# A two-block transformer layer on one core: the last product's second half of tokens delayed by two weight chunks, the norm's weights multiplied in during the product, two queues for the output, and the last expert and the gating unit written in another order

## The chip, the cores and the metric

One core of a Trainium2 chip runs the whole program in one launch. The metric is device time in microseconds (us), as the median of the runs shown. The engines are called PE (matmuls), DVE (vector), ACT (scalar, with function tables), POOL and SP; SP, ACT and POOL issue transfers (DMAs), each on a queue of its own.

## What is computed

Two transformer blocks in a row, on 256 tokens of width 2048, all in float32. The first block has four attention mixers and a mixture of 16 experts; the second a long convolution (hyena), a gating unit and a feed-forward part. The pieces that the change touches:

```python
# first block, experts: 4 groups of 4, each token in one group
y = (silu(h @ w_gate[e]) * (h @ w_up[e]) * weight[e]) @ w_down[e]      # D=2048, D_EXPERT=512

# second block, gating unit (D_SGU=1024, 8 heads, chunks of 128 tokens)
u, v = jnp.split(gelu(p), 2, axis=-1)
v = layernorm(v, ln_g, ln_b)
s = jnp.einsum('hpq,bnqhc->bnphc', w_s, v) + b_s
y_sgu = u * s

# the end
x = x + (silu(gate) * up) @ w_ffn_out       # D_FF=5632
return rmsnorm(x) * norm_final_g            # over the 2048 columns of a token
```

## The kernel before

Every large product is made of three matmuls in a 32-bit format with fewer mantissa bits (`mm3`, L160 to L162): a weight chunk of 128 x 1024 numbers is loaded on SP's queue (`rload`, L193, 512 KB), ACT makes its high part `whi` (L148), DVE the low part `wlo` (L151), and PE multiplies high by high, high by low and low by high. Loads go into a ring of five buffers (`wraw`), the parts into rings of three each (`nsplit`). Products of form "C" have the weights stationary and give columns by tokens; those of form "T" have the tokens stationary and give 128 tokens by 512 columns.

The text of the kernel is not the order of execution: a planner goes through the instructions by priority (their place in the text) and by when it expects their inputs, and writes one list for each engine. It takes a later instruction first where an earlier one isn't ready by its reckoning. On the chip each engine then follows its list strictly.

**Experts** (`experts`, L1149 on). For each of 16 experts: the gate product (8 chunks, `widen(wg)`), Silu, then the down product of the expert before (`down()`, 8 chunks, two halves of 1024 columns), then the up product (8 chunks), gate times up times weight (L1179), four transposes (L1182) and the split of the result. After the last expert its own `down()` follows at once.

**Gating unit** (`sgu`, L1575 on). ACT's queue loads the norm's weights `lg`, `lb`, the bias `bs` (each broadcast to 128 partitions, 512 KB) and `ws`. Two T products give v, with Gelu (L1590) and statistics (L1591). In the text there follow the eight transposes of `ws` (L1596), the root and the norm of v in passes over 1024 columns (L1605 to L1607), then two C products for u, and for each head the small products with `v` (L1616).

**The end** (`block2`, L1377, from L1454). `xt` holds the residual with tokens on partitions, `gb` the broadcast weights of the last norm. The product with `w_ffn_out` runs in four quarters of 512 columns; in a quarter each of its 22 chunks (two row blocks of weights) is multiplied for both halves of 128 tokens at once. After a quarter DVE adds (L1469) and ACT squares with a sum (L1471). After the fourth the root is taken (L1476), DVE multiplies by root and weights in eight passes of 512 columns (L1481), and SP stores each (L1482, 256 KB).

Of the kernel before, what the change touches and what calls it, by code (L numbers as in the profile page):

```python
# [9 lines left out]
F32 = mybir.dt.float32  # L10
F32R = mybir.dt.float32r
I32 = mybir.dt.int32
AF = mybir.ActivationFunctionType
# [5 lines left out]
P = 128  # L19
S = 256  # L20
D = 2048
KD = D // P
# [119 lines left out]
class Body:  # L142
# [53 lines left out]
    def wload(self, src, kt, width, perm=False):  # L196
# [9 lines left out]
        h = self.wp.tile([P, 1024], F32R, name="whi", tag="whi", bufs=self.nsplit)  # L206
        l = self.wp.tile([P, 1024], F32R, name="wlo", tag="wlo", bufs=self.nsplit)
# [137 lines left out]
    def run(self):  # L345
        ctx, tc, nc, i = self.ctx, self.tc, self.nc, self.i
        self.nraw, self.nsplit = 5, 3
        self.ahead, self.turn, self.more, self.nada, self.alias, self.taken, self.first = {}, None, None, 0, {}, 0, True
        self.const = ctx.enter_context(tc.tile_pool(name="const", bufs=1, reuse_waits="tile"))
# [799 lines left out]
    def experts(self, groups, weights, step, finish, between=None):  # L1149
# [7 lines left out]
        for n in range(4 * len(groups)):  # L1157
# [18 lines left out]
            if down:  # L1176
                down()
            u = widen(wu, "u")
            nc.vector.scalar_tensor_tensor(he, sg, cs[:, e:e + 1], u, OP.mult, OP.mult)  # L1179
            pt = self.bank("b").rearrange("p (k s) -> p k s", k=4)  # L1180
            for k in range(4):
                nc.tensor.transpose(pt[:, k], he[:, k * P:(k + 1) * P], self.ident)  # L1182
            hh, hl = (midr[:, j].rearrange("p (k s) -> p k s", k=4) for j in range(2))
            self.split(hh, hl, pt)
# [3 lines left out]
            def down(e=e, hh=hh, hl=hl, wd=wd, y=y, take=take):  # L1188
# [4 lines left out]
                for half in range(2):  # L1193
                    for k in range(4):
                        wt = self.wload(src[4 * half + k], 1, 1024)
                        for q in range(2):
                            self.mm3(y[half * 2 + q], (hh[:, k], hl[:, k]), [t[:, 0, q * 512:(q + 1) * 512] for t in wt],
                                     e == 0 and k == 0, e == 3 and k == 3)
                        step()
# [177 lines left out]
    def block2(self):  # L1377
# [59 lines left out]
        with ExitStack() as cf:  # L1437
# [26 lines left out]
            ss = fp.tile([P, 2, 8], F32, name="fss")  # L1464
            T2 = [("T", 0, 512, 0), ("T", 0, 512, 1)]
            for q in range(4):
                cs = slice(q * 512, (q + 1) * 512)
                for a, p in enumerate(self.gemm(i["w_ffn_out_2"][0], KF, q * 512, 512, lambda k: (ah[:, k], al[:, k]), T2)):
                    nc.vector.tensor_tensor(xt[:, a, cs], xt[:, a, cs], p, OP.add)  # L1469
                    sq = fp.tile([P, 512], F32, name="fsq", tag="fsig", bufs=1)  # L1470
                    nc.scalar.activation(sq, xt[:, a, cs], AF.Square, accum_out=ss[:, a, q:q + 1])  # L1471
            for a in range(2):
# [6 lines left out]
                for q in range(4):  # L1479
                    cs = slice(q * 512, (q + 1) * 512)  # L1480
                    nc.vector.scalar_tensor_tensor(xt[:, a, cs], xt[:, a, cs], r[:, 6:7], gb[:, cs], OP.mult, OP.mult)  # L1481
                    nc.sync.dma_start(self.out[0, a * P:(a + 1) * P, cs], xt[:, a, cs])  # L1482
# [92 lines left out]
    def sgu(self, w, xs, C4):  # L1575
# [3 lines left out]
        nc.scalar.dma_start(lg, bc("sgu_ln_g_2", DH))  # L1579
        nc.scalar.dma_start(lb, bc("sgu_ln_b_2", DH))  # L1580
        nc.scalar.dma_start(bs, bc("sgu_b_s_2", DH))
# [11 lines left out]
        for h0 in (0, 4):  # L1593
            ps = self.bank("b").rearrange("p (h q) -> p h q", h=4)
            for h in range(4):
                nc.tensor.transpose(ps[:, h], ws[:, h0 + h], self.ident)  # L1596
            nc.vector.tensor_copy(wst[:, h0:h0 + 4], ps)
        for a in range(2):
            r = sp.tile([P, 8], F32, name="sr", tag="sr", bufs=2)
            nc.vector.bn_aggr(r[:, :2], st[:, a].rearrange("p h s -> p (h s)"))  # L1600
            nc.vector.tensor_scalar(r[:, 2:3], r[:, 1:2], EPS, None, OP.add)
            nc.scalar.activation(r[:, 3:4], r[:, 2:3], AF.Sqrt)
# [45 lines left out]
```

## Time and profile before

| | us |
|---|---|
| median of three runs (lowest, highest) | 2630.53 (2626.57, 2633.94) |
| the profiled execution | 2630.51 |
| its span, first to last instruction | 2628.4 |
| PE busy in the span | 2551.8 (97%) |
| DVE busy | 1788.6 (68%) |
| ACT busy | 1333.8 (51%) |

All times in the rows are microseconds from the span's start unless marked ns. A timeline row gives start, duration, engine, line, operation and tiles; a number in brackets is the engine's idle time before it and what ended that. Matmuls overlap in the pipeline, so the distance of two starts says more than a duration.

### The profile page before, as it was taken

How to read it: one execution, taken by the hardware profiler on the slowest of the kernel's cores; microseconds unless marked ns; L12 is line 12 of the kernel's file. 1: busy time of each engine (PE TensorE's matmuls, PEld its weight loads, DVE VectorE, ACT ScalarE, POOL GpSimd, SP SyncE). 2: the span in 40 equal slices, each digit the busy share in tenths (PEclk: the TensorE clock that was granted, in tenths of full speed). 3: DMA queues.
4: the chain of work that ended last, by engine and by line, in shares of the span. 5: the costliest groups of instructions: out<-in, count | busy, mean ns of one | idle time of the engine just before them, and what ended most of it. 6: DMA issues, size and time to landing. Idle time of an engine off the chain costs nothing.

```text
span 2628.4 us, 43630 instructions
## 1 busy us (share of the span) xinstructions
PE 2551.8 (97%) x17355; PEld 2246.0 (85%) x17355; DVE 1788.6 (68%) x2513; ACT 1333.8 (51%) x1774; POOL 7.3 (0%) x21
## 2 busy tenths in 40 slices
PE   6998999998999999999999999999999999999997
PEld 2476878897888878787997899999999999998886
DVE  5647768777999899997787655556655555555444
ACT  2333444545777777776444444445544444443443
POOL 0000000000000000000000000000000000000000
PEclk8998999998999999999999999999999999999999
DMA  9998889883899999996554555555565555555554
GB/s 362 335 300 289 283 308 328 307 312 114 314 340 322 341 341 375 342 374 248 190 167 129 169 185 185 190 187 184 187 192 189 188 188 189 188 190 196 195 193 137
DMA packets 320394, 640.81 MB, mean 244 GB/s; under 512 B 21748, under 2 KB 36116, under 8 KB 319416
## 3 DMA queue, kind: packets, MB, share of 16 engines
q1 hardware_dynamic: 310768, 618.83, 69.2%
q10 hardware_dynamic: 8392, 13.89, 1.6%
q0 software_dynamic: 1024, 5.25, 0.6%
q8 instruction: 137, 2.24, 0.3%
q14 instruction: 73, 0.60, 0.1%
HBM read 631.02 MB, written 6.35 MB: 242 GB/s over the span
## 4 chain that ended last, share of the span: by engine, by line
PE 72%; DVE 2%; ACT 1%; issue 1%; DMA 0%; ACTq 0%; DVEq 0%
PE ps_y L160 19%; PE ps_y L161 19%; PE ps_y L162 19%; PE ps_u L161 2%; PE ps_g L161 2%; PE ps_g L160 2%; PE ps_u L162 2%; PE ps_u L160 2%; PE ps_g L162 2%; DVE wlo L151 1%; PE ps_b L160 0%; PE ps_b L161 0%; PE ps_b L162 0%; DMA ws<-in_sgu_w_s_dram 0%; ACT whi L148 0%
## 5 line engine op out<-in xcount | busy, mean ns | idle before, releaser
L151 DVE TENSOR_TENSOR wlo<-wraw,whi 128x1024 fp32r<-128x1024 f32 (+1 forms) x972 | 1163.8, 1205 | 642.7 <-ACT whi L148 614.5
L148 ACT ACTIVATE whi<-wraw 128x1024 fp32r<-128x1024 f32 (+1 forms) x972 | 1011.2, 1045 | 923.6 <-PE ps_y L161 453.3
L160 PE MATMUL ps_y<-hH,whi 128*128 128x256 f32 x2432 | 684.2, 281 | 0.0
L162 PE MATMUL ps_y<-hH,wlo 128*128 128x256 f32 x2432 | 680.0, 280 | 0.0
L161 PE MATMUL ps_y<-hL,whi 128*128 128x256 f32 x2432 | 679.2, 279 | 0.0
L160 PEld LDWEIGHTS ps_y<-hH,whi 128*128 128x128 f32 x2432 | 457.8, 188 | 1.9 <-issue 1.7
L161 PEld LDWEIGHTS ps_y<-hL,whi 128*128 128x128 f32 x2432 | 457.8, 188 | 1.9 <-issue 1.7
L162 PEld LDWEIGHTS ps_y<-hH,wlo 128*128 128x128 f32 x2432 | 457.8, 188 | 1.5 <-issue 1.3
L160 PE MATMUL ps_mm<-hH,whi 128*128 128x256 f32 (+1 forms) x784 | 226.4, 289 | 4.7 <-ACT whi L148 4.7
L162 PE MATMUL ps_mm<-hH,wlo 128*128 128x256 f32 (+1 forms) x784 | 222.6, 286 | 2.2 <-DVE wlo L151 2.1
L161 PE MATMUL ps_mm<-hL,whi 128*128 128x256 f32 (+1 forms) x784 | 221.6, 283 | 0.0
L160 PEld LDWEIGHTS ps_mm<-hH,whi 128*128 128x128 f32 (+1 forms) x784 | 147.1, 188 | 24.8 <-issue 11.6
L162 PEld LDWEIGHTS ps_mm<-hH,wlo 128*128 128x128 f32 (+1 forms) x784 | 146.6, 188 | 10.3 <-DVE wlo L151 5.6
L161 PEld LDWEIGHTS ps_mm<-hL,whi 128*128 128x128 f32 (+1 forms) x784 | 147.2, 188 | 1.1 <-issue 0.6
L161 PE MATMUL ps_y<-wlo,actH 128*128 128x512 f32 x352 | 137.5, 390 | 0.0
L162 PE MATMUL ps_y<-whi,actL 128*128 128x512 f32 x352 | 137.3, 390 | 0.0
L160 PE MATMUL ps_y<-whi,actH 128*128 128x512 f32 x352 | 137.2, 390 | 0.0
L161 PE MATMUL ps_y<-wlo,piece 128*128 128x512 f32 x256 | 101.8, 398 | 0.3 <-DVE wlo L151 0.2
L162 PE MATMUL ps_y<-whi,piece 128*128 128x512 f32 x256 | 100.1, 392 | 0.3 <-DVE piece L151 0.3
L480 PE MATMUL ps_ada<-piece,cact 128*32 128x512 f32 x488 | 88.6, 641 | 5.1 <-DMA piece<-in_ada_w_dram 4.2
L160 PE MATMUL ps_y<-whi,piece 128*128 128x512 f32 x256 | 91.4, 392 | 0.7 <-ACT piece L148 0.7
L484 DVE SCALAR_TENSOR_TENSOR arow<-piece,cs,arow 128x512 f32<-128x512 f32 x120 | 89.5, 746 | 1.8 <-DMA piece<-in_ada_w_dram 0.8
(521 smaller groups left out, 3885.9 us busy)
## 6 DMA issues: line engine op xcount, KB each, us to landing
wraw<-in_w_in_dram SPq DMA_DIRECT2D x224, 512.0 KB, 4.2
piece<-in_ada_w_dram SPq DMA_DIRECT2D x186, 512.0 KB, 7.0
wraw<-in_w_ffn_in_dram SPq DMA_DIRECT2D x176, 512.0 KB, 4.5
wraw<-in_exp_w_down_dram SPq DMA_DIRECT2D x125, 512.0 KB, 5.6
wraw<-in_exp_w_up_dram SPq DMA_DIRECT2D x124, 512.0 KB, 5.5
wraw<-in_exp_w_gate_dram SPq DMA_DIRECT2D x122, 512.0 KB, 5.4
wraw<-in_w_ffn_out_dram SPq DMA_DIRECT2D x88, 512.0 KB, 4.2
wraw<-in_w_out_dram SPq DMA_DIRECT2D x64, 512.0 KB, 4.8
```

Of the source, the lines that this page charges most:

```text
L148: self.nc.scalar.activation(dst, src, AF.Copy)
L151: self.nc.vector.tensor_tensor(dst, src, h.bitcast(F32), OP.subtract)
L160: mm(ps, a[0], b[0], start=start, stop=False)
L161: mm(ps, a[0], b[1], start=False, stop=False)
L162: mm(ps, a[1], b[0], start=False, stop=stop)
L480: nc.tensor.matmul(ps[m:m + 32], self.cact[:, k], r, start=q == 0, stop=q == 3)
L484: nc.vector.scalar_tensor_tensor(sb, r, self.cs[:, k:k + 1], sb, OP.mult, OP.add)
```

## The change

It has four parts. In the gating unit the three broadcast loads move to POOL's queue, and root, norm of v and transposes of ws become a generator, one step of which is written behind each chunk of the first u product. For the last expert, the down product of the one before is written behind its up product, and the transposes and the split of the last expert's result behind two of that product's chunks. In the last quarter of the final product the second 128 tokens follow the first by two chunks, with two more buffers for each split part (`split_more`, taken for two chunks in five); the first 128 tokens are closed when their sum is complete. The weights of the last norm are multiplied in after each quarter, into `xg`, which lies where `xT` was; the close is one pass of 1024 columns on DVE and one on ACT, each stored from its own queue (SP, ACT). A root of no use is written ahead of the product.

```diff
@@ -203,8 +203,15 @@
         else:
             raw = self.ahead.pop(self.turn) if self.turn in self.ahead else self.rload(src, kt, n)
             self.turn += 1
-        h = self.wp.tile([P, 1024], F32R, name="whi", tag="whi", bufs=self.nsplit)
-        l = self.wp.tile([P, 1024], F32R, name="wlo", tag="wlo", bufs=self.nsplit)
+        pool, tag, bufs = self.wp, "", self.nsplit
+        if self.split_more:
+
+            here, at = self.split_more
+            self.split_more = here, (at + 1) % (bufs + 2)
+            if at < 2:
+                pool, tag, bufs = here, "2", 2
+        h = pool.tile([P, 1024], F32R, name="whi", tag="whi" + tag, bufs=bufs)
+        l = pool.tile([P, 1024], F32R, name="wlo", tag="wlo" + tag, bufs=bufs)
         if perm:
             for a in range(2):
                 g = lambda t, pat, **kw: t[:, :n].rearrange(pat, k=kt, a=2, i=4)
@@ -346,6 +353,7 @@
         ctx, tc, nc, i = self.ctx, self.tc, self.nc, self.i
         self.nraw, self.nsplit = 5, 3
         self.ahead, self.turn, self.more, self.nada, self.alias, self.taken, self.first = {}, None, None, 0, {}, 0, True
+        self.split_more = None
         self.const = ctx.enter_context(tc.tile_pool(name="const", bufs=1, reuse_waits="tile"))
         self.res = ctx.enter_context(tc.tile_pool(name="res", bufs=1, reuse_waits="tile"))
         self.wp = ctx.enter_context(tc.tile_pool(name="wts", bufs=1, reuse_waits="tile"))
@@ -1173,19 +1181,28 @@
                 mid, midr = (t.rearrange("p (a n) -> p a n", a=2) for t in between)
             sg, he = mid[:, 0], mid[:, 1]
             nc.scalar.activation(sg, g, AF.Silu)
-            if down:
+            hh, hl = (midr[:, j].rearrange("p (k s) -> p k s", k=4) for j in range(2))
+
+            def turned():
+                pt = self.bank("b").rearrange("p (k s) -> p k s", k=4)
+                for k in range(4):
+                    nc.tensor.transpose(pt[:, k], he[:, k * P:(k + 1) * P], self.ident)
+                self.split(hh, hl, pt)
+
+
+            ends = n == 4 * len(groups) - 1 and not between
+            if down and not ends:
                 down()
             u = widen(wu, "u")
             nc.vector.scalar_tensor_tensor(he, sg, cs[:, e:e + 1], u, OP.mult, OP.mult)
-            pt = self.bank("b").rearrange("p (k s) -> p k s", k=4)
-            for k in range(4):
-                nc.tensor.transpose(pt[:, k], he[:, k * P:(k + 1) * P], self.ident)
-            hh, hl = (midr[:, j].rearrange("p (k s) -> p k s", k=4) for j in range(2))
-            self.split(hh, hl, pt)
+            if ends:
+                down(midst=turned)
+            else:
+                turned()
             if e == 0:
                 y = []
 
-            def down(e=e, hh=hh, hl=hl, wd=wd, y=y, take=take):
+            def down(e=e, hh=hh, hl=hl, wd=wd, y=y, take=take, midst=None):
                 if e == 0:
                     finish()
                     y += [self.bank("y") for _ in range(4)]
@@ -1196,6 +1213,8 @@
                         for q in range(2):
                             self.mm3(y[half * 2 + q], (hh[:, k], hl[:, k]), [t[:, 0, q * 512:(q + 1) * 512] for t in wt],
                                      e == 0 and k == 0, e == 3 and k == 3)
+                        if midst and half == 0 and k == 1:
+                            midst()
                         step()
                     if e == 3:
                         take(half, y[2 * half:2 * half + 2])
@@ -1462,24 +1481,58 @@
                         nc.tensor.transpose(ps[:, kk * P:(kk + 1) * P], self.xT[:, q * 4 + kk, a * P:(a + 1) * P], self.ident)
                     nc.vector.tensor_copy(xt[:, a, q * 512:(q + 1) * 512], ps)
             ss = fp.tile([P, 2, 8], F32, name="fss")
+
+            nc.scalar.activation(ss[:, 0, 7:8], rB[:, 0:1], AF.Sqrt)
             T2 = [("T", 0, 512, 0), ("T", 0, 512, 1)]
-            for q in range(4):
-                cs = slice(q * 512, (q + 1) * 512)
-                for a, p in enumerate(self.gemm(i["w_ffn_out_2"][0], KF, q * 512, 512, lambda k: (ah[:, k], al[:, k]), T2)):
-                    nc.vector.tensor_tensor(xt[:, a, cs], xt[:, a, cs], p, OP.add)
-                    sq = fp.tile([P, 512], F32, name="fsq", tag="fsig", bufs=1)
-                    nc.scalar.activation(sq, xt[:, a, cs], AF.Square, accum_out=ss[:, a, q:q + 1])
-            for a in range(2):
+            wo, ks = i["w_ffn_out_2"][0], lambda k: (ah[:, k], al[:, k])
+
+            def add(q, a, p):
+
+                t = xt[:, a, q * 512:(q + 1) * 512]
+                nc.vector.tensor_tensor(t, t, p, OP.add)
+                sq = fp.tile([P, 512], F32, name="fsq", tag="fsig", bufs=1)
+                nc.scalar.activation(sq, t, AF.Square, accum_out=ss[:, a, q:q + 1])
+                nc.vector.tensor_tensor(xg[:, a, q * 512:(q + 1) * 512], t, gb[:, q * 512:(q + 1) * 512], OP.mult)
+
+            def close(a):
+
                 r = ss[:, a]
                 nc.vector.tensor_reduce(r[:, 4:5], r[:, :4], AX.X, OP.add)
                 nc.vector.tensor_scalar(r[:, 4:5], r[:, 4:5], 1.0 / D, EPS, OP.mult, OP.add)
                 nc.scalar.activation(r[:, 5:6], r[:, 4:5], AF.Sqrt)
                 nc.vector.reciprocal(r[:, 6:7], r[:, 5:6])
                 self.newton(r[:, 6:7], r[:, 4:5], r[:, 7:8])
-                for q in range(4):
-                    cs = slice(q * 512, (q + 1) * 512)
-                    nc.vector.scalar_tensor_tensor(xt[:, a, cs], xt[:, a, cs], r[:, 6:7], gb[:, cs], OP.mult, OP.mult)
-                    nc.sync.dma_start(self.out[0, a * P:(a + 1) * P, cs], xt[:, a, cs])
+                rows, cs = slice(a * P, (a + 1) * P), [slice(h * 1024, (h + 1) * 1024) for h in range(2)]
+                nc.vector.tensor_scalar(xg[:, a, cs[0]], xg[:, a, cs[0]], r[:, 6:7], None, OP.mult)
+                nc.sync.dma_start(self.out[0, rows, cs[0]], xg[:, a, cs[0]])
+                nc.scalar.activation(xg[:, a, cs[1]], xg[:, a, cs[1]], AF.Copy, scale=r[:, 6:7])
+                nc.scalar.dma_start(self.out[0, rows, cs[1]], xg[:, a, cs[1]])
+
+
+            xg = self.xT.rearrange("p k s -> p (k s)").rearrange("p (a d) -> p a d", a=2)
+            for q in range(3):
+                for a, p in enumerate(self.gemm(wo, KF, q * 512, 512, ks, T2)):
+                    add(q, a, p)
+
+            self.split_more = fp, 0
+            ps = self.accumulators(T2)
+            held = {}
+            for c in range(KF // 2 + 2):
+                if c < KF // 2:
+                    k0 = 2 * c
+                    held[c] = self.wload(wo[k0 * P:(k0 + 2) * P, 1536:].rearrange("(k p) n -> p k n", p=P), 2, 512)
+                for a, n in ((0, c), (1, c - 2)):
+                    if not 0 <= n < KF // 2:
+                        continue
+                    for kk in range(2):
+                        k = 2 * n + kk
+                        x = [t[:, a * P:(a + 1) * P] for t in ks(k)]
+                        self.mm3(ps[a], x, [t[:, kk] for t in held[n]], k == 0, k == KF - 1)
+                if c == KF // 2 - 1:
+                    add(3, 0, ps[0])
+                    close(0)
+            add(3, 1, ps[1])
+            close(1)
 
 
     def hyena(self, w, xs, C4):
@@ -1576,9 +1629,9 @@
         nc, sp, i = self.nc, self.sp, self.i
         bc = lambda nm, n: bass.AP(tensor=i[nm].tensor, offset=i[nm].offset, ap=[[0, P], [1, n]])
         lg, lb, bs = (sp.tile([P, DH], F32, name=n) for n in ("lng", "lnb", "sbs"))
-        nc.scalar.dma_start(lg, bc("sgu_ln_g_2", DH))
-        nc.scalar.dma_start(lb, bc("sgu_ln_b_2", DH))
-        nc.scalar.dma_start(bs, bc("sgu_b_s_2", DH))
+        nc.gpsimd.dma_start(lg, bc("sgu_ln_g_2", DH))
+        nc.gpsimd.dma_start(lb, bc("sgu_ln_b_2", DH))
+        nc.gpsimd.dma_start(bs, bc("sgu_b_s_2", DH))
         ws = sp.tile([P, 8, P], F32, name="ws")
         nc.scalar.dma_start(ws, i["sgu_w_s_2"][0].rearrange("h p q -> p h q"))
         v = sp.tile([P, 2, DH], F32, name="sv")
@@ -1590,23 +1643,36 @@
                 nc.scalar.activation(v[:, a, cs], p, AF.Gelu, scale=self.tr12[:, a:a + 1])
                 nc.vector.bn_stats(st[:, a, hf], v[:, a, cs])
         wst = sp.tile([P, 8, P], F32, name="wst")
-        for h0 in (0, 4):
-            ps = self.bank("b").rearrange("p (h q) -> p h q", h=4)
-            for h in range(4):
-                nc.tensor.transpose(ps[:, h], ws[:, h0 + h], self.ident)
-            nc.vector.tensor_copy(wst[:, h0:h0 + 4], ps)
-        for a in range(2):
-            r = sp.tile([P, 8], F32, name="sr", tag="sr", bufs=2)
-            nc.vector.bn_aggr(r[:, :2], st[:, a].rearrange("p h s -> p (h s)"))
-            nc.vector.tensor_scalar(r[:, 2:3], r[:, 1:2], EPS, None, OP.add)
-            nc.scalar.activation(r[:, 3:4], r[:, 2:3], AF.Sqrt)
-            nc.vector.reciprocal(r[:, 4:5], r[:, 3:4])
-            self.newton(r[:, 4:5], r[:, 2:3], r[:, 5:6])
-            nc.vector.tensor_scalar(v[:, a], v[:, a], r[:, 0:1], r[:, 4:5], OP.subtract, OP.mult)
-            nc.vector.tensor_tensor(v[:, a], v[:, a], lg, OP.mult)
-            nc.vector.tensor_tensor(v[:, a], v[:, a], lb, OP.add)
+
+        def chores():
+
+            rs = []
+            for a in range(2):
+                r = sp.tile([P, 8], F32, name="sr", tag="sr", bufs=2)
+                nc.vector.bn_aggr(r[:, :2], st[:, a].rearrange("p h s -> p (h s)"))
+                nc.vector.tensor_scalar(r[:, 2:3], r[:, 1:2], EPS, None, OP.add)
+                nc.scalar.activation(r[:, 3:4], r[:, 2:3], AF.Sqrt)
+                nc.vector.reciprocal(r[:, 4:5], r[:, 3:4])
+                self.newton(r[:, 4:5], r[:, 2:3], r[:, 5:6])
+                rs.append(r)
+            yield
+            for a in range(2):
+                nc.vector.tensor_scalar(v[:, a], v[:, a], rs[a][:, 0:1], rs[a][:, 4:5], OP.subtract, OP.mult)
+                nc.vector.tensor_tensor(v[:, a], v[:, a], lg, OP.mult)
+                yield
+                nc.vector.tensor_tensor(v[:, a], v[:, a], lb, OP.add)
+                yield
+            for h0 in (0, 4):
+                ps = self.bank("b").rearrange("p (h q) -> p h q", h=4)
+                for h in range(4):
+                    nc.tensor.transpose(ps[:, h], ws[:, h0 + h], self.ident)
+                nc.vector.tensor_copy(wst[:, h0:h0 + 4], ps)
+            yield
+        bg = chores()
         for hf in range(2):
-            for m, p in enumerate(self.gemm(w, KD, 3072 + hf * 512, 512, xs, C4)):
+            for m, p in enumerate(self.gemm(w, KD, 3072 + hf * 512, 512, xs, C4, lambda _: next(bg, None))):
+                if m == 0:
+                    self.drain(bg)
                 h = hf * 4 + m
                 u = sp.tile([P, S], F32, name="su", tag="su", bufs=2)
                 nc.vector.tensor_tensor(u, p, self.rB, OP.mult)
```

## Rows read from the trace of the kernel before

**Rows 1.** The page's first part: busy time, share of the span, instructions.

```profile
PE 2551.8 (97%) x17355; PEld 2246.0 (85%) x17355; DVE 1788.6 (68%) x2513; ACT 1333.8 (51%) x1774; POOL 7.3 (0%) x21
```

**Rows 2.** Waits of PE, whole span: waited for, us in total, times, longest.

```profile
PE ps_g L1596 <- DMA ws<-in_sgu_w_s_dram: 4.6, 1, 4.6
...
PE ps_g L1616 <- DVE sv L1607: 2.3, 1, 2.3
```

**Rows 3.** Timeline around the transposes of ws: start, duration, what, idle before.

```profile
1433.44 0.35 ACTq L1579 DMA_DIRECT2D lng<-in_sgu_ln_g_dram  x1
...
1434.79 0.57 ACTq L1583 DMA_DIRECT2D ws<-in_sgu_w_s_dram  x1
...
1445.46 1.12 PE L1596 MATMUL ps_g<-vec,ws 128*128 128x128 f32 x4 [4.58 <-DMA ws<-in_sgu_w_s_dram]
...
1446.62 0.69 DVE L1597 COPY wst<-ps_g 128x512 f32<-128x512 f32 x1 [7.69 <-PE ps_g L1596]
...
1451.31 0.39 PE L160 MATMUL ps_y<-whi,hH 128*128 128x512 f32 x1
```

**Rows 4.** DMA issues: count, KB each, median us from issue to landing.

```profile
wraw<-in_w_in_dram SPq DMA_DIRECT2D x224, 512.0 KB, 4.2
...
lng<-in_sgu_ln_g_dram ACTq DMA_DIRECT2D x1, 512.0 KB, 6.5
...
sbs<-in_sgu_b_s_dram ACTq DMA_DIRECT2D x1, 512.0 KB, 8.8
```

**Rows 5.** Window behind that wait: length, busy by engine, granted clock, DMA share, GB/s.

```profile
1445.00:1447.00 2.00, 1.53 (x7) 1.54 (x8) 0.38 (x1) 0.00 (x0) 0.00 (x0) 0.50 0.00 0
```

**Rows 6.** Timeline around the norm of v, and the later small products.

```profile
1469.32 1.54 DVE L1605 TENSOR_SCALAR sv<-sv,sr 128x1024 f32<-128x1024 f32 x2
...
1474.41 0.46 PE L1616 MATMUL ps_g<-wst,sv 128*128 128x128 f32 x2 [2.35 <-DVE sv L1607]
...
1478.23 0.28 PE L162 MATMUL ps_y<-hH,wlo 128*128 128x256 f32 x1
...
1516.63 0.61 PE L1616 MATMUL ps_u<-wst,sv 128*128 128x128 f32 x4
...
1518.33 0.36 PE L160 MATMUL ps_y<-hH,whi 128*128 128x256 f32 x1
```

**Rows 7.** Timeline of PE behind the last expert's up product.

```profile
1196.32 0.39 PE L162 MATMUL ps_u<-whi,piece 128*128 128x512 f32 x1
...
1197.55 0.66 PE L1182 MATMUL ps_b<-vec,piece 128*128 128x128 f32 x4 [0.84 <-DVE piece L1179]
...
1200.99 0.39 PE L160 MATMUL ps_y<-whi,piece 128*128 128x512 f32 x1
```

**Rows 8.** Timeline from the last matmul on.

```profile
2614.04 0.39 PE L162 MATMUL ps_y<-whi,actL 128*128 128x512 f32 x1
...
2615.98 1.28 ACT L1476 ACT_TABLE_LOAD   x1
...
2616.19 0.15 DVE L1475 TENSOR_SCALAR fss<-fss 128x1 f32<-128x1 f32 x1
2617.28 0.30 ACT L1476 ACTIVATE fss<-fss 128x1 f32<-128x1 f32 x2
...
2618.48 5.39 DVE L1481 SCALAR_TENSOR_TENSOR hH<-hH,fss,hL 128x512 f32<-128x512 f32 x8
```

**Rows 9.** Windows over the stores, columns as in rows 5.

```profile
2619.00:2620.00 1.00, 0.00 (x0) 0.00 (x0) 1.00 (x3) 0.00 (x0) 0.00 (x0) 0.50 0.00 0
2620.00:2621.00 1.00, 0.00 (x0) 0.00 (x0) 1.00 (x2) 0.00 (x0) 0.00 (x0) 0.50 0.88 334
...
2626.00:2627.00 1.00, 0.00 (x0) 0.00 (x0) 0.00 (x0) 0.00 (x0) 0.00 (x0) 0.50 0.31 117
```

**Rows 10.** One chunk's split in the final product, timelines of DVE and ACT.

```profile
2438.76 1.23 DVE L151 TENSOR_TENSOR wlo<-wraw,whi 128x1024 fp32r<-128x1024 f32 x1 [1.49 <-ACT whi L148]
...
2440.38 1.06 ACT L148 ACTIVATE whi<-wraw 128x1024 fp32r<-128x1024 f32 x1 [1.66 <-PE ps_y L162]
```

## The prediction

> **What bounds the kernel now.** I read the page's busy table first, then the waits of the matmul engine (PE) over the whole span, then the timeline around each wait that falls in a place the diff touches, then the windows for the granted clock and the transfer rate. PE is busy for 97% of the span [rows 1]. So time can come only from gaps in PE's stream and from what follows its last matmul. Two of the largest gaps lie in the gating unit: 4.6 us until the tile ws has landed and 2.3 us until the normalised v is there [rows 2]. Instructions do not run in the order in which they are written: the transposes of ws stand behind both v products in the text, and they ran in the middle of the second one [rows 3]. An engine then follows its own list strictly, and whatever waits at its head holds up the rest.
>
> **The gating unit, first stall.** The three broadcast loads and ws go out on ACT's queue, from 1433.44 to 1434.79, and PE waits for ws until 1445.46, from 1440.88 on [rows 3]. Behind the transposes, on DVE, stands the copy of wst, and behind that the low parts of the weights, so the next product can't go on either. While this lasts the clock falls to 0.50 [rows 5]. From 1440.88 to 1451.31 PE does eight transposes and nine matmuls of the product. Twelve matmuls of this shape take a chunk of 2.72 us at full clock [rows 10], so nine are 2.04; four transposes span 0.66 [rows 7], eight at most 1.3, and I take 1.2. So 10.43 - 3.2 = 7.2 us are lost here.
>
> The change puts ws first on ACT's queue and the three others on POOL's, which does nothing else at this time. The first load of the queue now lands after 6.5 us, the third after 8.8, a weight load after 4.2 [rows 4]. Issued at 1433.44, ws lands at 1437.6 by the last figure, at 1442.2 by the second; I take 6.8, a little over the first because three loads run beside it: 1440.2. If the transposes keep their place, they then find ws there, but the copy of 0.69 us still stands ahead of a low part of 1.23 on DVE [rows 3, 10], which leaves about 1.3 us of wait. So 7.2 - 1.3 = 5.9 are gained. Bounds: 7.2 if the transposes move behind the product, where the text now has them; 3.2 if they come one chunk earlier and wait about 2.3 us, with the 1.7 us that a fall of the clock costs after a wait of that length (below); nothing if the four loads, 2 MB in all, finish together at 1445, where the last of them does now.
>
> On that landing the Trainium skill (DMA: Bandwidth & Descriptors, Issuing engines are not separate DMA queues) speaks against the move: transfers from SP, ACT and POOL share the same 16 engines and interleave, so another queue adds no bandwidth. By that rule alone the last bound would hold, and the whole would come to about 2621 us. No row here shows a load of ACT's beside POOL's.
>
> **Second stall.** DVE works on v in one block from 1469.32 until PE gets it at 1474.41, and no low part is made in that time; PE has stopped at 1472.06 [rows 6]. From there to 1478.23 it does sixteen small products, which later take 1.70 us at full clock, and three matmuls, 0.35: 6.17 - 2.05 = 4.1 us lost [rows 6], 2.35 of it idle and the rest, 1.7, at the fallen clock. The change deals the v work out over the chunks of the next product. DVE has 1.49 us free in a chunk [rows 10], a pass over 1024 columns is about 1.2, so the passes fit between the low parts, though tightly: from 1469.3 to 1480.6 DVE would have no gap at all. I leave 0.7 us for a late low part and take 3.4. Bounds: 4.1 and 1. The loads of lng, lnb and sbs are first wanted at 1470 or later, so that even 30 us to landing cost nothing.
>
> **The last expert.** Its up product ends at 1196.55; then gate times up, four transposes and their split stand alone on the path, and PE reaches 1200.99 having done four transposes (0.5) and six matmuls (1.36) [rows 7]. So 4.44 - 1.9 = 2.5 us are lost. The other fifteen experts have the next gate product to cover this. The change lets the down product of the expert before run there: after two of its chunks, 2.7 us, the transposes come, and the multiplication of 0.75 behind at most one low part of 1.23 is done by then. Six more chunks cover the split. No transfer is added; two groups of loads change places on SP's queue. I take 2.4; bounds 1 and 2.6.
>
> **The tail.** Call the end of the last matmul T (2614.43 now). The first output pass starts at T+4.05, the eighth ends at 2623.87, and the span ends 4.53 later, at T+13.97 [rows 8]. New: the first 128 tokens finish three half chunks, 4.1 us, before T, so their sum, root and stores run beside the last eighteen matmuls. For the second 128 tokens the chain to the root is the same, but without the table load. Of its 1.28 us only what lies behind the sum's scaling (ended 2616.34) counts, 0.92 [rows 8]: the factor is there at T+3.13. Then one pass of 1024 columns on DVE (0.77, [rows 6]) and one on ACT (1.06, [rows 10]) side by side, and stores at T+3.95 and T+4.25. Now the first pass ends at 2619.22 and bytes flow from 2620, 0.8 us later, at 334 GB/s; in the window from 2626 only 117 GB/s are left, 0.35 us of work, so the last byte has passed 2.05 us before the end [rows 8, 9]. One MB at that rate is 3.2: 3.95 + 0.8 + 3.2 + 2.05 = T+10.0, a gain of 3.9. I take 3.7. Bounds: 2.5 (0.8 for the early root, below, and 0.6 for stores that cross the first half's) and 5.3 (if SP's half has passed before ACT's flows: 4.25 + 0.8 + 1.6 + 2.05 = T+8.7).
>
> The table load itself is where row and page differ. The row has 1.28 us and the root's start right behind it, at 2617.28. The Trainium skill (ScalarE: Activation LUTs, What ACT_TABLE_LOAD costs) adds a drain and comes to about 2.66 us a switch; by that figure the tail would gain 1.4 more and the forecast be 2613.7.
>
> Costed at nothing: eight multiplications by the norm's weights, some 0.67 us each [rows 8], at quarter ends. DVE's 1.49 us a chunk [rows 10] and two chunks of split weights hide them; without that cover they cost 2.7 at the end. The early root: one small ACT instruction. If it is run long before (its input is ready after the norm, and only then do the Silu groups come), the table is switched back and the load returns, but in the first half's close, where the last matmuls hide most of it: up to 0.8 us. The two added pairs of split buffers: five pairs, three of them alive, leave two chunks of lead, as three with one alive do now.
>
> **Sum.** 5.9 + 3.4 + 2.4 + 3.7 = 15.4 us. The profiled execution took 2630.51 us with a span of 2628.4, and the median of the runs is 2630.53, so the same 2.1 us lie around it: 2628.4 - 15.4 + 2.1 = **2615.1 us**.
>
> **The rivals.**
> 1. *ws is still waited for.* For: with a shorter wait for ws its transposes may be put earlier, and the traffic beside it is new. Against: they stand where the planner saw a gap in PE's list for late parts, and what makes those late does not move. 3.2 in place of 5.9 gives 2617.8; nothing, with ws landing near 1445, 2621.0.
> 2. *The gating unit's stalls only move.* DVE has as much work as before, and its copy of wst or a late low part stops PE elsewhere for as long. For: 11 us without a DVE gap. Against: every low part has a chunk of lead, and the first two thirds of a chunk's matmuls don't need it. Then only the 6.1 us of the last expert and the tail come: 2624.4, no measurable difference.
> 3. *Slower: the delayed half starves the last quarter.* If the held chunks leave no buffer free, each split (1.06 + 1.23 and two hand-overs, about 2.4 us) is exposed in some twenty chunks: 48 us, less the 15: 2664. It decides from 1.1 us a chunk on. Five pairs speak against it.
> 4. *The early root does not hold its table:* 2615.9, inside the first case.
>
> **How the numbers follow.** All four terms about as summed (2611 to 2619): 0.55. Rival 1: 0.25. Rival 2: 0.16. Rival 3: 0.04. What a measurement of this kernel can tell from no change is about 0.3%, 7.9 us. The first case and rival 1 lie beyond it: faster 0.80. Rival 2 is the same: 0.16. Slower: 0.04. The sum of the best bounds is 7.2 + 4.1 + 2.6 + 5.3 = 19.2, so 2611.3; with some of the scatter of the runs shown (4 us each way) the low end is 2609. The high end takes in rival 1 and most of rival 2: 2625.
>
> **What would show it.** Right: no wait of PE on ws over 1 us, and a clock at 1.00 from 1432 to 1480; no wait on v; no wait of the down product on its transposed input near 1197; about 10 us from the last matmul to the end, with no table load among them. Wrong: transposes of ws ahead of its landing, PE waiting on low parts between 1466 and 1490, on split weights in the last 65 us, or stores that take over 6 us after the last pass.

## The result, and the profile after

The changed kernel takes 2616.59 us (median of 13 runs, 2611.24 to 2623.52). The kernel before took 2633.61 in 13 runs beside them. The ratio is 0.9936, with a 95% interval of 0.9923 to 0.9949: 13.4 to 20.3 us, faster by more than 0.3%. The prediction was 2615.1, a gain of 15.4.

The profiled execution took 2617.88 us with a span of 2616.0, so 12.4 less in the span than before. The first part of its page answers to [rows 1]:

```profile
PE 2554.0 (98%) x17355; PEld 2245.3 (86%) x17355; DVE 1789.2 (68%) x2515; ACT 1336.2 (51%) x1777; POOL 9.0 (0%) x24
```

PE does the same 17355 matmuls, in the same time within 2.2 us. What went is idle time. To see where, I cut the span at matmuls that both kernels have and took the starts from the views of single tiles:

| stretch, us | before | after | gained | forecast |
|---|---|---|---|---|
| start to the first gate product of the experts | 634.8 | 636.1 | -1.3 | 0 |
| to the last sum of squares behind the experts (L1297, now L1316) | 604.0 | 605.6 | **-1.6** | +2.4 |
| to the last product of the convolution | 189.8 | 189.9 | -0.1 | 0 |
| to the last small product of the gating unit (L1616, now L1682) | 89.7 | 77.8 | **+11.9** | +9.3 |
| to the end of the span | 1110.1 | 1106.6 | **+3.5** | +3.7 |

The first line is scatter: with nothing changed ahead of the experts they began between 634.0 and 646.2 in the profiles of this study. The other lines sum to 13.7. Most stretches repeat within 0.3 us where the text of their part is the same, with two exceptions. The gating unit of the kernel before took 87.3 to 89.7 in the five profiles that have it unchanged, and the stretch with the reordered last expert 604.3 to 605.7 in five. So +11.9 may be as little as 9.5 and -1.6 as little as -0.3.

**Gating unit.** The timeline of the changed kernel, picked from the loads, the transposes and the first small product:

```profile
1420.70 0.55 POOL L1632 DMA_DIRECT2D lng<-in_sgu_ln_g_dram  x1 [57.10 <-ACT yfH L148]
...
1432.29 0.53 POOL L1634 DMA_DIRECT2D sbs<-in_sgu_b_s_dram  x1 [10.49 <-PE ps_b L162]
...
1436.36 0.40 ACTq L1636 DMA_DIRECT2D ws<-in_sgu_w_s_dram  x1
...
1477.05 0.60 PE L1668 MATMUL ps_u<-vec,ws 128*128 128x128 f32 x4
...
1477.49 0.60 PE L1668 MATMUL ps_b<-vec,ws 128*128 128x128 f32 x4
1477.69 0.69 DVE L1669 COPY wst<-ps_u 128x512 f32<-128x512 f32 x1 [1.03 <-PE ps_u L1668]
...
1483.53 0.61 PE L1682 MATMUL ps_g<-wst,sv 128*128 128x128 f32 x4
```

And its windows over the same place (columns as in [rows 5]):

```profile
1430.00:1450.00 20.00, 20.00 (x96) 16.63 (x95) 13.07 (x20) 11.06 (x15) 0.53 (x1) 1.00 0.67 210
1450.00:1470.00 20.00, 20.00 (x130) 18.09 (x129) 14.22 (x27) 10.61 (x13) 0.00 (x0) 1.00 0.56 168
1470.00:1490.00 20.00, 20.00 (x175) 20.00 (x175) 16.77 (x26) 10.45 (x15) 0.00 (x0) 1.00 0.60 194
```

PE is busy throughout at full clock; no wait on ws or v is left. But the transposes ran 41 us after the issue of ws, not 10.7 as in [rows 3]: they left the v products altogether. And lng was issued 11.6 us ahead of sbs, 15.7 ahead of ws, so the four loads hardly met: sbs landed 3.9 us after its issue, before ws went out.

**Last expert.** The changed kernel's timeline, picked from POOL, PE and ACT:

```profile
1185.26 0.66 POOL L1583 DMA_DIRECT2D kft<-kf_d  x1 [621.94 <-DMA wraw<-in_exp_w_down_dram]
...
1189.05 0.60 PE L1189 MATMUL ps_b<-vec,piece 128*128 128x128 f32 x4
...
1198.27 1.06 ACT L148 ACTIVATE whi<-wraw 128x1024 fp32r<-128x1024 f32 x1 [2.07 <-DMA wraw<-in_exp_w_down_dram]
...
1200.64 0.50 PE L161 MATMUL ps_y<-wlo,piece 128*128 128x512 f32 x1 [0.53 <-DVE wlo L151]
...
1202.79 2.14 ACT L148 ACTIVATE whi<-wraw 128x1024 fp32r<-128x1024 f32 x2 [1.09 <-DMA wraw<-in_exp_w_down_dram]
...
1203.01 0.50 PE L161 MATMUL ps_y<-wlo,piece 128*128 128x512 f32 x1 [0.53 <-DVE wlo L151]
```

The transposes run without the wait of [rows 7]. But ACT now waits 3.2 us for down weights, as it never did here before, and PE for low parts behind it.

**Tail.** The changed kernel's timeline, which answers to [rows 8]:

```profile
2602.52 0.69 DVE L1492 TENSOR_TENSOR hH<-hH,ps_y 128x512 f32<-128x512 f32 x1 [4.61 <-PE ps_y L162]
...
2603.98 1.28 ACT L1502 ACT_TABLE_LOAD   x1
...
2606.24 0.40 PE L162 MATMUL ps_y<-whi,actL 128*128 128x512 f32 x1
...
2606.48 1.15 ACT L1508 ACTIVATE xT<-xT,fss 128x1024 f32<-128x1024 f32 x1 [1.00 <-DVE fss L277]
2606.67 0.69 DVE L1492 TENSOR_TENSOR hH<-hH,ps_y 128x512 f32<-128x512 f32 x1 [0.23 <-PE ps_y L162]
...
2607.53 0.62 ACT L1494 ACTIVATE fsq<-hH 128x512 f32<-128x512 f32 x1
...
2607.94 0.68 DVE L1495 TENSOR_TENSOR xT<-hH,hL 128x512 f32<-128x512 f32 x1
...
2608.54 0.15 DVE L1500 TENSOR_REDUCE fss<-fss 128x1 f32<-128x4 f32 x1
...
2610.12 0.75 DVE L1506 TENSOR_SCALAR xT<-xT,fss 128x1024 f32<-128x1024 f32 x1
...
2611.29 0.35 ACTq L1509 DMA_DIRECT2D out_dram<-xT  x1
```

Windows over the last stores, as in [rows 9]:

```profile
2612.00:2613.00 1.00, 0.00 (x0) 0.00 (x0) 0.00 (x0) 0.00 (x0) 0.00 (x0) 0.50 0.99 406
2613.00:2614.00 1.00, 0.00 (x0) 0.00 (x0) 0.00 (x0) 0.00 (x0) 0.00 (x0) 0.50 1.04 426
2614.00:2615.00 1.00, 0.00 (x0) 0.00 (x0) 0.00 (x0) 0.00 (x0) 0.00 (x0) 0.50 0.25 98
```

From the start of the last matmul to the end are 9.8 us, where there were 14.4. Of these 4.6, 1.1 went elsewhere: the 264 matmuls of the last quarter start 0.231 us apart, those of the two quarters ahead of it, and of the last quarter before, 0.2267.

### The profile page after: what moved, and what is told of

Read it like the earlier page. It is cut to its first block, busy times and chain, and to the rows that moved or that the text cites. A ratio compares the mean times of both kernels' runs of the same rounds, so it can differ in the third digit from the quotient of the medians.

```text
span 2616.0 us, 43634 instructions
## 1 busy us (share of the span) xinstructions
PE 2554.0 (98%) x17355; PEld 2245.3 (86%) x17355; DVE 1789.2 (68%) x2515; ACT 1336.2 (51%) x1777; POOL 9.0 (0%) x24
## 4 chain that ended last, share of the span: by engine, by line
PE 72%; DVE 2%; ACT 1%; issue 1%; DMA 0%; ACTq 0%; DVEq 0%
PE ps_y L160 19%; PE ps_y L161 19%; PE ps_y L162 19%; PE ps_u L161 2%; PE ps_g L161 2%; PE ps_g L160 2%; PE ps_u L162 2%; PE ps_u L160 2%; PE ps_g L162 2%; DVE wlo L151 1%; DMA wraw<-in_exp_w_down_dram 0%; PE ps_b L160 0%; PE ps_b L161 0%; PE ps_b L162 0%; ACT whi L148 0%
## 5 line engine op out<-in xcount | busy, mean ns | idle before, releaser
L160 PEld LDWEIGHTS ps_mm<-hH,whi 128*128 128x128 f32 (+1 forms) x784 | 147.5, 188 | 24.6 <-issue 11.6
L162 PEld LDWEIGHTS ps_mm<-hH,wlo 128*128 128x128 f32 (+1 forms) x784 | 146.8, 188 | 10.7 <-DVE wlo L151 5.9
```

Source lines behind the costliest of these rows:

```text
L160: mm(ps, a[0], b[0], start=start, stop=False)
L162: mm(ps, a[1], b[0], start=False, stop=stop)
```

## The experiments

**One part alone: the last expert, and what it starts.** The loads of the convolution's filter (kft, on POOL) wait for buffers that the down weights leave. With the down product earlier they begin at 1185.26; before it was 1194.56. `e_exp` is the kernel before with the reordered last expert alone. `e_late` is the kernel before with the first two filter loads of 1 MB (one for each of the two kft tiles) held behind a copy into their tile that DVE does after the experts; the small loads of 256 KB are not held. `e_exp_late` has both, `a_late` is the changed kernel with the hold.

```diff
+            ends = n == 4 * len(groups) - 1 and not between
...
+            if ends:
+                down(midst=turned)
```

```diff
+        if o == 0:
+            nc.vector.tensor_copy(kf[:, 0, 0:1], self.rB[:, 0:1])
```

> The expert part alone. The stretch from the first gate product to the last sum of squares takes 604.0 us before and 605.6 in the changed kernel. Theory A (the wait of 2.5 us is gone, but the filter loads of the hyena stage, 2.3 MB on POOL's queue, now start 9 us earlier and take the transfer engines from the last down weights): the stretch is 605 to 606.5, PE or ACT wait for a down weight, the whole 0 to 2 us slower. Theory B (my step: 2.4 us gained; the loss in the changed kernel's profile is scatter): the stretch is 601.6, the whole 2.4 faster.

> The kernel before with only the filter loads held back. Both theories: the stretch stays at 604.0, since the wait of 2.5 us behind the last up product is still there; under 603.5 would say that the filter loads cost the kernel before something too.

> The expert part, with the first two filter loads held back until the second block's norm factor is there (about 1249 us), 70 us before they are used. Theory A: no wait for a down weight, the stretch 601 to 602, the whole some 2.5 us faster than before and 3 to 4 faster than the expert part alone. Theory B: no different from the expert part alone.

> The changed kernel with the filter loads held back. Theory A: the stretch falls from 605.6 to about 602, and the whole is 3 to 4 us faster than the changed kernel: 2613 us, 20 faster than before on the same chip. Theory B: no gain on the changed kernel.

| | median us | ratio to before (95%) | experts' stretch |
|---|---|---|---|
| e_exp | 2633.26 | 0.9999 (0.9986 to 1.0013) | 604.6 |
| e_late | 2641.06, one run | | 604.0 |
| e_exp_late | 2630.14 | 0.9989 (0.9976 to 1.0002) | 602.5 |
| a_late | 2615.84 | 0.9935 (0.9921 to 0.9950) | 602.4 |

The timed ratios can't separate 2 us here; the stretch can. It took 604.0 to 604.2 us in the six profiles with the old order, 604.3 to 605.7 in the five with the new one, and 602.4 to 602.6 in the three with the new one and the hold. So the reorder alone gives nothing (604.6 against 604.0, a little under the 605 to 606.5 that theory A expected and 3.0 over theory B's 601.6), the hold alone nothing (604.0), both together 1.5, and the hold takes 3.2 off the changed kernel (1.7 to 3.3 over all profiles). The 3 to 4 us on the whole that `a_late` was expected to gain on the changed kernel are not shown by its timed ratio. What the two do to the transfers is in the DMA view of nine microseconds, in the changed kernel from 1189 to 1198 (the first number behind a queue is its packets, the second its MB; q0 is POOL's, q1 SP's):

```profile
q0 software_dynamic: 350, 2.30, 61.7%
q1 hardware_dynamic: 399, 1.44, 40.4%
...
wraw<-in_exp_w_down_dram SPq DMA_DIRECT2D x7, 512.0 KB, 11.5
```

in the kernel before in the same nine:

```profile
q1 hardware_dynamic: 974, 3.50, 97.9%
```

and in `a_late` from 1187 to 1196:

```profile
q1 hardware_dynamic: 770, 2.80, 86.9%
q0 software_dynamic: 182, 0.49, 14.6%
...
wraw<-in_exp_w_down_dram SPq DMA_DIRECT2D x7, 512.0 KB, 6.0
```

The filter took 2.30 MB of 3.74, and the down weights landed 11.5 us after their issue in place of 6.0. In `a_late` the two held loads go at 1266 (L1585; L1587 is a small one, not held), and ACT's waits for down weights are gone:

```profile
1190.29 0.57 POOL L1587 DMA_DIRECT2D kft<-kf_d  x1
1266.63 1.05 POOL L1585 DMA_DIRECT2D kft<-kf_d  x2 [75.77 <-DVE kft L1584]
```

The convolution does not miss them: from the experts to its last product `a_late` takes 189.8 us, as before.

**The gating unit: queue, landing or order.** `e_q` is the kernel before with the three broadcasts on POOL's queue and nothing else; `e_sgu` has the whole gating-unit part; `a_actq` is the changed kernel with the broadcasts back on ACT's queue; `e_wsfirst` is the kernel before with ws ahead of the broadcasts on ACT's queue.

```diff
-        nc.scalar.dma_start(lg, bc("sgu_ln_g_2", DH))
+        nc.gpsimd.dma_start(lg, bc("sgu_ln_g_2", DH))
...
```

```diff
+        ws = sp.tile([P, 8, P], F32, name="ws")
+        nc.scalar.dma_start(ws, i["sgu_w_s_2"][0].rearrange("h p q -> p h q"))
         nc.scalar.dma_start(lg, bc("sgu_ln_g_2", DH))
...
```

> The kernel before with only the three broadcast loads moved to POOL's queue; text and order else as before. By the step of the prediction (the transposes keep their place, ws lands 4.6 us after its issue, a part of the wait remains): the stretch falls from 89.7 by about 5.9, to 84, and the wait for v stays. If only the order counted: 89.7, with the wait for ws as long as before. If the wait went wholly: 82.5.

> The gating unit's part alone (three loads on POOL's queue, the norm of v dealt out, the transposes late). The stretch from the last matmul of the hyena stage to the last small product of the unit takes 89.7 us before and 77.8 in the changed kernel. If the parts add up: 78, the whole 11 to 12 us faster than before, no wait on ws or v. By the sum of the prediction: 80.4 and 9.3. If the gain hung on another part: over 82.

> The changed kernel with the three broadcast loads back on ACT's queue ahead of ws. The transposes now run 40 us after the loads. If the order of the text does it all: the stretch stays at 77.8 to 78.5 though ws lands at about 1445. If the move of the loads is needed: the transposes or the norm of v wait, and the stretch is over 80.

> The kernel before, with one edit: the load of ws goes out ahead of the three broadcasts on ACT's queue. All engines but ACT have the same lists of instructions as in the kernel before, so this is the landing of ws alone, with no new order around it. Theory A, that of the prediction's own step (with the transposes of ws in their old place, only the time of landing counts): ws lands 4.5 to 7 us after its issue, so near 1440 on the scale of the kernel before, the wait of 4.6 us for it falls under 1.5 us, the clock stays up, and the stretch from the last product of the convolution to the last small product of the gating unit falls from 89.7 us to 82.5 to 85 (the wait on v of 2.3 us stays). Theory B, that the gain of the queue move came from the new order alone: the wait moves to wst or to a late low part of a weight at the same place, and the stretch stays within 1 us of 89.7. Theory C: both waits go, as they did when the broadcasts changed queues, and the stretch is near 78.

| | us | gating unit's stretch | transposes of ws, us behind the convolution's last product | waits of PE there |
|---|---|---|---|---|
| before | | 89.7 | 16.8 | ws 4.6, v 2.3 |
| e_wsfirst | 2634.11, one run | 85.3 | 12.1 | low part 2.8, v 2.3 |
| a_actq | 2623.9, one run | 83.0 | 15.9 | ws 3.7, low part 1.0 |
| e_q | 2624.3, one run | 77.9 | 28.7 | none |
| e_sgu | 2621.29, ratio 0.9950 (0.9929 to 0.9970) | 77.8 | 45.5 | none |
| after | 2616.59 | 77.8 | 45.5 | none |

(The single times carry the scatter of the first 640 us; the stretch is the measure. Its new form took 77.8 or 77.9 in all seven profiles that have no wait there; its old form scatters, and gains against it are good to about 2 us.) In `e_wsfirst` ws lands 6.1 us after its issue. Its expectation has one thing wrong: PE's list in this stretch is the same as before's, DVE's is not. Swapping the loads alone made the planner write there (- before, + `e_wsfirst`):

```
+L1597 COPY wst<-ps_g 128x512
+L1597 COPY wst<-ps_b 128x512
 L1591 BN_STATS sst<-sv 128x6 x2
-L1597 COPY wst<-ps_g 128x512
-L151 TENSOR_TENSOR wlo<-wraw,whi 128x1024 x3
-L1597 COPY wst<-ps_b 128x512
```

and its timeline shows what that costs:

```profile
1441.43 0.40 ACTq L1580 DMA_DIRECT2D ws<-in_sgu_w_s_dram  x1
...
1448.72 0.60 PE L1596 MATMUL ps_g<-vec,ws 128*128 128x128 f32 x4
...
1449.35 0.69 DVE L1597 COPY wst<-ps_g 128x512 f32<-128x512 f32 x1 [6.08 <-PE ps_g L1596]
...
1449.96 0.68 DVE L1597 COPY wst<-ps_b 128x512 f32<-128x512 f32 x1
1450.56 1.28 DVE L1591 BATCH_NORM_STATS2 sst<-sv 128x6 f32<-128x512 f32 x2
1451.75 2.34 DVE L151 TENSOR_TENSOR wlo<-wraw,whi 128x1024 fp32r<-128x1024 f32 x2
...
1453.02 0.50 PE L161 MATMUL ps_y<-wlo,hH 128*128 128x512 f32 x1 [2.79 <-DVE wlo L151]
```

DVE sits idle for 6.1 us with the copy of wst at the head of its list, while the statistics, which the kernel before did first, stand behind it. Two copies and two statistics then come ahead of the low part that PE needs: 2.4 us, and a wait of 2.8. So ws without a wait was worth 4.4 us of the 7.2, and the order on DVE held back 2.8. In `e_q` nothing is held back, and its 77.9 lies outside all that was expected of it (84, 89.7 or 82.5). Its text has transposes and norm as before, yet the planner wrote the transposes so that they ran some 12 us later in the stretch, the copies of wst on either side of the last statistics, and low parts between the passes of v, as DVE's timeline of `e_q` shows:

```profile
1461.75 1.23 DVE L151 TENSOR_TENSOR wlo<-wraw,whi 128x1024 fp32r<-128x1024 f32 x1 [1.54 <-ACT whi L148]
1462.89 0.69 DVE L1591 BATCH_NORM_STATS2 sst<-sv 128x6 f32<-128x512 f32 x1
...
1467.75 0.81 DVE L1605 TENSOR_SCALAR sv<-sv,sr 128x1024 f32<-128x1024 f32 x1
...
1468.55 1.21 DVE L151 TENSOR_TENSOR wlo<-wraw,whi 128x1024 fp32r<-128x1024 f32 x1
1469.67 1.22 DVE L1606 TENSOR_TENSOR sv<-sv,lng 128x1024 f32<-128x1024 f32 x1
```

Three moved lines brought 11.8 of the 11.9 us, and the rewritten text adds nothing that shows to that. Without the queue move (`a_actq`) the rewriting is worth 6.7: v's wait goes, but the transposes stand early and wait. By these numbers it is the place in the list, and not the earlier landing, that ends the wait for ws in `e_q`: in the kernel before, ws had landed 16.8 us behind the convolution's last product even on ACT's queue, and `e_q` wants it after 28.7. No run has the list of `e_q` with the loads on ACT's queue, so this is argued and not shown. Why the planner took another order was not looked into.

**The tail: pace, delay, table.** `e_tail` is the kernel before with the change of the last product alone. `a_nolag` is the changed kernel with both halves of the tokens at the same chunk, `a_root` with the early root tied to the tokens' tile, and `a_late_root` with that and the hold of the filter loads.

```diff
-            for c in range(KF // 2 + 2):
+            for c in range(KF // 2):
...
-                for a, n in ((0, c), (1, c - 2)):
+                for a, n in ((0, c), (1, c)):
```

```diff
-            nc.scalar.activation(ss[:, 0, 7:8], rB[:, 0:1], AF.Sqrt)
+            nc.vector.tensor_tensor(ss[:, 0, 7:8], xt[:, 1, D - 1:D], xt[:, 1, D - 1:D], OP.mult)
+            nc.scalar.activation(ss[:, 0, 7:8], ss[:, 0, 7:8], AF.Sqrt)
```

> The last product's part alone. From the last small product of the gating unit to the end: 1110.1 us before, 1106.6 in the changed kernel, where the way from the last matmul to the end is 4.6 shorter and the matmuls of the last quarter start every 0.231 us in place of 0.2267, 1.1 us in all. If the parts add up: 1106.6, the whole 3.5 us faster than before. By the prediction: 1106.4.

> The changed kernel, with the two halves of the tokens at the same weight chunk in the last quarter (no delay of two chunks); the two added pairs of split buffers stay. Theory A (the delay is worth the sums and stores of the first half): the time from the last matmul's start to the end grows from 9.8 us to 11.5 to 13; the spacing of the matmuls in the last quarter falls back from 0.231 to 0.227 us if the alternation of the chunks slowed them (1.1 us in all), and stays at 0.231 if it was something else that the edit brought. Rival (the gain of the tail came from the products with the norm's weights taken in early and from the two store queues, not from the delay): it stays within 0.7 us of 9.8.

> The changed kernel, with the early square root taken from a multiplication of the tokens' own tile after the norm, so that it can't run before the last product begins. Theory A (the early root ran before the Silu groups, so its table was lost and a load of 1.28 us came back in the first half's close, beside matmuls): no table load stands in the last 20 us, the first half's passes begin about 1 us earlier, and the time from the last matmul's start to the end falls from 9.8 us by 0.0 to 0.5, since the end hangs on the second half's chain. Theory B (the load in the close delays ACT's stores of the first half so far that the second half's stores queue behind them): it falls by 1 us or more.

> The changed kernel, with the early root tied as in the run before, and with the convolution's filter loads held back until after the experts. If the filter loads ahead of the last down weights were what ate the last expert's gain, the stretch from the first gate product to the last sum of squares is 602.4 us again in place of 605.6, the whole 3 to 3.7 us faster than the changed kernel, near 2613, and the ratio to the kernel before 0.991 to 0.994. Rival: the run of this form seen before fell there by chance, and the stretch is 604 to 606.

| | us | last matmul's start to end | spacing in the last quarter |
|---|---|---|---|
| before | | 14.4 | 0.2267 |
| e_tail | 2629.63, ratio 0.9985 (0.9972 to 0.9999) | 9.5 | 0.2310 |
| after | 2616.59 | 9.8 | 0.2310 |
| a_nolag | 2618.33, one run | 12.8 | 0.2287 |
| a_root | 2626.28, one run | 9.4 | 0.2310 |
| a_late_root | 2616.83, ratio 0.9935 (0.9913 to 0.9958) | 9.4 | 0.2310 |

(The same tail took 9.7 us in `a_late` and 9.5 in `a_actq`.) The delay is worth 3.0 us at the end, and 2.5 with its slower pace: from the gating unit's last small product to the end `a_nolag` took 1109.1 us, the changed kernel 1106.6, the kernel before 1110.1. What is left of the change, the early multiplication, the longer passes and the two queues, is worth the other 1.6 at the end; they were not taken apart. The pace of `a_nolag` is the surprise. There the matmuls of a chunk stand in the order of the kernel before, and only the two added pairs of split buffers are left of the change; still three chunks of every five run at 0.229 to 0.231 us and two at 0.2267, in step with the rotation of the five pairs. So the pace does not come from the order of the halves alone. Which reads of the added buffers cost it was not tried.

In `a_root` the table load stands at the start of the product, beside idle time of ACT, and none is left in the last 20 us:

```profile
2381.41 1.28 ACT L1486 ACT_TABLE_LOAD   x1
2382.70 0.20 ACT L1486 ACTIVATE fss<-fss 128x1 f32<-128x1 f32 x1
```

Its last matmul starts at 2615.03, and the second half's pass 3.5 us later, where the changed kernel takes 3.88 (2606.24 to 2610.12):

```profile
2618.53 0.75 DVE L1507 TENSOR_SCALAR xT<-xT,fss 128x1024 f32<-128x1024 f32 x1
```

`a_late_root` keeps both gains in its profile (experts' stretch 602.6, tail 9.4, 3.3 us less than the changed kernel from the first gate product on). Its six runs spread over 8.8 us, and their interval covers the changed kernel's ratio, so it isn't shown to be faster.

The three parts add up: the ratios of `e_exp`, `e_sgu` and `e_tail` multiply to 0.9934, and the whole change measured 0.9936.

## Why the prediction held, point by point

The sum was 15.4, the stretches give 13.7, the timed medians 17.0 with an interval of 13.4 to 20.3. The total was right, its parts less so, and that is in part luck: the last expert came out 4.0 us under its term and the gating unit 2.6 over, and these two misses have separate causes.

**First stall, 5.9, and second, 3.4.** Together 11.9 in place of 9.3. The step "if the transposes keep their place" named the condition, and it didn't hold: they went behind the v products, which was the upper bound of 7.2, and the norm's passes fitted between low parts with no wait, the upper bound of 4.1. These make 11.3; the last 0.6 is not assigned and lies within the scatter of the old form. Nor is the price of the fallen clock, 1.7 in the second stall, a fixed one. `e_exp_late` has the same lists here as the kernel before and the same wait of 2.3 us for v, but the granted clock stayed at 1.00 behind it (from 1472 to 1476), where it was 0.70 and 0.50 before (from 1474 to 1478). It came back earlier behind the first stall too, and the stretch was 2.4 us shorter in all. With the transposes in their place, `e_wsfirst` measured 4.4, not 5.9: ws was there after 6.1 us (6.8 taken) and not waited for, but ahead of the low part I had put one copy of 0.69, and the new list had two and two statistics. Rival 1 (still waiting for ws) came true only in `a_actq`, where the broadcasts stayed on ACT's queue; rival 2 (the stalls only move) in part, in `e_wsfirst`.

The bound of no gain supposed that the four loads finish together. They hardly met: ws went out when the three others had landed, and landed 4.6 us after its issue, the first broadcast 4.2 after its own. So the rule of the Trainium skill (DMA: Bandwidth & Descriptors, Issuing engines are not separate DMA queues) that another queue adds no bandwidth was not put to the test at this place. Where two queues did load at once, at the last expert, the rule agrees with the trace: with POOL's 2.30 MB, SP's queue moved 1.44 MB in nine microseconds, where it had moved 3.50 in the same nine before.

**Last expert, 2.4.** This is the step that failed: -1.6 in the changed kernel, and no gain in any of the five profiles with the new order and no hold. The stall went as forecast, but "no transfer is added; two groups of loads change places" overlooked that an earlier down product frees buffers earlier, and that 2.3 MB of filter loads on another queue were waiting for them. I had counted the edit's own transfers and not those that its buffers gate. With those held back the reorder is worth 1.5 (`e_exp_late`); the other 0.9 of the forecast is not assigned.

**Tail, 3.7.** 3.5, as the difference of two misses. The path from the last matmul gained 4.6, as its end came 9.8 us after the start of the last matmul: the last stores ran at 406 and 426 GB/s, where 334 was taken. Against that the factor was there 0.35 us later than forecast, at T+3.48 for T+3.13: the second half's square stood behind ACT's pass over the first (2606.48 to 2607.63), and its sum behind DVE's multiplication by the norm's weights (2607.94 to 2608.62). Both come of the table load, which put off the first half's close; with the root tied, the factor was there at T+3.09. The other miss is that "costed at nothing" left out 1.1 for the slower pace of the last quarter. The delayed half starved nothing: PE has no wait in the whole product, so rival 3 is out.

**Early root.** Rival 4 came true: the root ran at 1880.1, ahead of the Silu groups, whose own table load starts at 1890.1, and the load came back in the first half's close. Tying the root was worth 0.4 on the way to the last passes in both runs that have it, where "up to 0.8" stood; of the whole way to the end 0.1 to 0.4, as the tail scatters. The row has 1.28 us for the load, and the root 0.01 behind it in `a_root`. The 2.66 a switch of the Trainium skill (ScalarE: Activation LUTs, What ACT_TABLE_LOAD costs) shows in no row here.

## What to carry to other kernels

Where a planner orders the instructions, an edit acts through the lists that it writes: compare the lists before pricing a wait, since here three moved lines brought some 10 to 12 us and a swap of loads undid part of its own gain. An instruction moved ahead frees its buffers ahead, so list the transfers on every queue that wait for those buffers, and hold back those that are needed late. For gains of a few microseconds in a span with scatter of ten, cut the profile at matmuls common to both kernels and compare stretches.

## What the hardware showed that was not expected

The spacing of matmuls with 512 columns is 0.2267 us at a granted clock of 1.00, and 0.231 at the same clock in the last quarter, where the split weights rotate through two added buffer pairs and the halves are apart; no wait marks the difference. With the same lists and the same wait of 2.3 us the granted clock fell to 0.50 in one execution (the kernel before) and stayed at 1.00 in another (`e_exp_late`). Stores of 512 KB from two queues moved 406 and 426 GB/s, where stores of 256 KB from one had moved 297 to 381 in the full microseconds of the kernel before; whether the queues or the size did it was not tried. And the first 640 us of the program, unchanged throughout, scatter by 12 us between executions, as much as the largest part of this change gave.
